# A two-block transformer on one core: roots by a GpSimd power and one Newton step, mask and residual adds on VectorE, norms at a higher priority

## The chip, the core and the metric

The kernel runs on one core of a Trainium2 chip. The core has a matrix engine (TensorE, PE in the profile), a vector engine (VectorE, DVE), an engine for activations and casts (ScalarE, ACT), GpSimd (POOL) and a sequencer that issues most of the loads (SyncE, SP). They run their own instruction queues in order and wait for each other by semaphores. The metric is the time of one execution on the device in microseconds (us), lower is better.

## The reference

The input is 256 tokens and 256 context tokens of 1024 features in float32. Two blocks run one after the other, and each has two layers:

```python
def first_block(...):                       # h_lat, h_ctx: [256, 1024] each
    for i in range(2):
        a = _modulate(_rms_norm(h, norm_mix[i]), m[0], m[1])
        o = _rwkv_mamba_mixer(a) if i == 0 else _neighbourhood_attention(a, rpb)
        h = h + m[2] * o
        t = _modulate(_rms_norm(h, norm_ffn[i]), m[3], m[4])
        h = h + m[5] * (_swiglu(t) if i == 0 else _moe_swiglu(t))   # 8 experts, top 2
    return _rms_norm(h_lat, norm_final)

def second_block(...):
    for i in range(2):
        u = modulate(h, sh1, sc1)           # layer norm, scale, shift
        y = (conv and differential attention if i == 0 else fourier_mix)(u) @ w
        h = layer_norm_affine(ALPHA * h + g1 * y, ln_g[i, 0], ln_b[i, 0])
        h = layer_norm_affine(ALPHA * h + g2 * sq_relu_mlp(modulate(h, sh2, sc2)),
                              ln_g[i, 1], ln_b[i, 1])
    return h
```

Each norm needs (x + eps) ** -0.5 for each token. In the neighbourhood attention a token sees a window of columns; outside it a mask takes the place of the bias.

## The kernel before

Tokens lie on the 128 partitions, so a residual h is four tiles of 128x1024 (two of context, two of tokens; after the attention only the last two go on). All products are done in three passes of single-precision parts (`mm3`, L231 to L233: high by high, low by high, high by low). Weights are loaded by SP into `raw` tiles of 128x1024; `split` makes the high part `wh` by a cast on ACT (L186) and the low part `wl` by a subtraction on DVE (L187). The same `split` makes xH and xL of the activations.

**A norm.** `norm_tile` (L416) squares the tile on ACT with a running sum `ms` (first block, L422), or takes mean and variance on DVE by `stats` (second block, L406 and L407), calls `rsqrt`, and scales the tile to `xn` on DVE (L423 or L426). `rsqrt` (L167) runs wholly on DVE: a first value from the bits (L173 to L175), then three Newton steps of two operations (L178 and L182; with n = 4 three operations, L180 to L182). With n = 1 it is nine operations of 128x1, each needing the one before. `xT` (L439) transposes two xn tiles on PE, applies scale and shift on the way out of PSUM (`xTf`, one half on ACT, the other on DVE, L453 and L454), and splits them. PE's first product of the next layer waits for that.

**Where norms stand after the mixer:** four at the mixer's end (`mixer_out`), four at the end of the first FFN (`l0_ffn`, w2 at f = 10), two at the attention's end, whose roots also scale the MoE's router, two for the context of the second block, `l1_end` (L1718) with two roots a tile, one root with n = 4 in the differential attention (L2086), and `post_norm` (L1914) with a layer norm in place and then the next layer's norm, two roots a tile, at three ends; at the last end of the program it has one root a tile.

**Adds on POOL.** In `l0_ffn` at f = 9 four tiles of 128x1024 are added to h (L1425). In `l1_attn`, `load_bias` (L1448) loads a `raw` tile of relative biases by 8 DMAs on SP, and POOL adds the mask `nam` (L1458), eight tiles in all; the mask comes by a DMA on POOL's queue (L1443). In `moe_pass`, after expert 6, POOL multiplies two accumulators by the gate (L1881) and adds them to h (L1882). POOL's queue also issues the loads of gates (L395) and of the rows `br` of ln_g and ln_b (L1901).

**What sets the order.** A scheduler places every engine's instructions by priority (in the main the order of the code; `high_priority` moves a stretch ahead by an offset) and by a simulated time at which operands are ready. On the engine they then run in exactly that order. Tiles come from pools with a fixed number of buffers; a new tile waits for the readers of the one that it replaces.

## Time and profile before

| | us |
|---|---|
| runs of the kernel before | 2846.43, 2853.15, 2857.51 |
| their median | 2853.15 |
| span of the profiled execution (first to last instruction) | 2849.6 |
| PE busy | 2636.1 (93%) |
| DVE busy | 1916.4 (67%) |
| ACT busy | 1286.7 (45%) |
| POOL busy | 191.2 (7%) |
| mean granted clock of PE | 0.945 of full speed |

The profile is of one execution. A timeline row begins with its start and its duration; "x5" is five instructions in a row, whose durations stand as one; the square bracket is the idle time of that engine before the row, and after the arrow stands the instruction whose end released it. A wait is idle time of an engine put down to the releaser that came last. Buffer numbers are left out of names: `xn`, `h`, `raw`, `sm` (any small tile). A wait costs time only on an engine that has nothing else to do.

### The profile page before, as it was taken

The page shows a single profiled execution, that of the slowest core. Times are in us where ns is not written, and L with a number is a line of the kernel's source. Part 1 is how long each engine was busy: PE and PEld are TensorE (multiplying, and loading weights), DVE is VectorE, ACT ScalarE, POOL GpSimd, SP SyncE. Part 2 cuts the span into 40 slices and gives each one's busy share as a digit, 9 for nine tenths or more (in the row PEclk, how much of TensorE's full clock was granted, in tenths as well). Part 3 has the DMA queues.
Part 4 walks back from the last instruction along what each step waited for, and adds up shares of the span by engine and source line. Part 5 has one row for each costly group of instructions (what it writes and reads, how often), then busy time and mean ns, then how long its engine had stood idle before and what let it go on. Part 6 is the DMA issues. An engine that isn't in the chain of part 4 may idle for free. (4 is left out here: it accounts for less than half of the span.)

```text
span 2849.6 us, 40766 instructions
## 1 busy us (share of the span) xinstructions
PE 2636.1 (93%) x15434; PEld 2092.5 (73%) x15434; DVE 1916.4 (67%) x3186; ACT 1286.7 (45%) x1760; POOL 191.2 (7%) x260
## 2 busy tenths in 40 slices
PE   6999899997999997999899999999997987996798
PEld 3775456654888886887788888888876766995797
DVE  4647778644544458345898988988896567556655
ACT  3532122112332223444688777778664443442343
POOL 0112223210000012000000000000010000000000
PEclk8999898888999998999899999999999998998899
DMA  6325776668333233333599999999986334653452
GB/s 235 93 67 177 256 243 208 196 226 296 97 96 96 89 92 87 103 91 108 198 375 349 342 350 345 361 359 333 367 315 228 113 96 141 188 182 99 155 185 74
DMA packets 324444, 570.83 MB, mean 200 GB/s; under 512 B 61752, under 2 KB 167608, under 8 KB 324240
## 3 DMA queue, kind: packets, MB, share of 16 engines
q1 hardware_dynamic: 304064, 544.61, 56.7%
q10 hardware_dynamic: 16784, 11.74, 1.4%
q0 software_dynamic: 3392, 11.80, 1.3%
q8 instruction: 123, 2.02, 0.3%
q14 instruction: 81, 0.66, 0.1%
HBM read 563.79 MB, written 4.28 MB: 199 GB/s over the span
## 5 line engine op out<-in xcount | busy, mean ns | idle before, releaser
L187 DVE TENSOR_TENSOR wl<-raw,wh 128x1024 fp32r<-128x1024 f32 x828 | 998.0, 1238 | 432.5 <-ACT wh L186 411.4
L186 ACT CAST wh<-raw 128x1024 fp32r<-128x1024 f32 x828 | 837.1, 1050 | 510.6 <-issue 193.0
L231 PE MATMUL ws<-xH,wh 128*128 128x256 f32 (+1 forms) x1392 | 458.5, 331 | 1.1 <-DVE xTf L454 0.8
L233 PE MATMUL ws<-xH,wl 128*128 128x256 f32 (+1 forms) x1392 | 457.3, 329 | 0.9 <-DVE wl L187 0.9
L232 PE MATMUL ws<-xL,wh 128*128 128x256 f32 (+1 forms) x1392 | 456.1, 328 | 0.5 <-DVE xL L187 0.5
L232 PE MATMUL mw<-wl,eH 128*128 128x512 f32 (+1 forms) x768 | 290.0, 378 | 2.6 <-DVE wl L187 2.4
L231 PEld LDWEIGHTS ws<-xH,wh 128*128 128x128 f32 x1392 | 265.5, 192 | 35.8 <-issue 10.1
L233 PEld LDWEIGHTS ws<-xH,wl 128*128 128x128 f32 x1392 | 265.1, 190 | 31.3 <-issue 6.8
L231 PE MATMUL mw<-wh,eH 128*128 128x512 f32 (+1 forms) x768 | 285.9, 375 | 1.1 <-ACT wh L186 1.1
L233 PE MATMUL mw<-wh,eL 128*128 128x512 f32 (+1 forms) x768 | 286.2, 373 | 0.0
L232 PEld LDWEIGHTS ws<-xL,wh 128*128 128x128 f32 x1392 | 265.3, 191 | 25.8 <-issue 2.5
L358 PE MATMUL ada<-raw,act 128*32 128x512 f32 x768 | 177.9, 734 | 33.3 <-DMA raw<-in_ada_w 12.8
L232 PEld LDWEIGHTS mw<-wl,eH 128*128 128x128 f32 x768 | 145.1, 189 | 35.0 <-DVE wl L187 11.0
L231 PEld LDWEIGHTS mw<-wh,eH 128*128 128x128 f32 x768 | 144.9, 189 | 27.2 <-ACT wh L186 2.0
L233 PEld LDWEIGHTS mw<-wh,eL 128*128 128x128 f32 x768 | 145.2, 189 | 24.2
L232 PE MATMUL y<-wl,uH 128*128 128x512 f32 x352 | 141.1, 401 | 4.0 <-DVE wl L187 4.0
L233 PE MATMUL y<-wh,uL 128*128 128x512 f32 x352 | 136.5, 392 | 0.0
L448 PE MATMUL xT<-ident,xn 128*128 128x128 f32 x160 | 36.7, 402 | 103.0 <-DVE xn L426 58.0
L231 PE MATMUL y<-wh,uH 128*128 128x512 f32 x352 | 115.5, 391 | 0.0
L448 PEld LDWEIGHTS xT<-ident,xn 128*128 128x128 f32 x160 | 29.7, 210 | 111.6 <-DVE xn L426 60.4
L358 PEld LDWEIGHTS ada<-raw,act 128*32 128x32 f32 x768 | 28.2, 123 | 110.8 <-issue 38.7
L231 PE MATMUL o<-wh,mH 128*128 128x512 f32 x256 | 100.0, 390 | 0.0
(475 smaller groups left out, 4182.8 us busy)
## 6 DMA issues: line engine op xcount, KB each, us to landing
raw<-in_moe_w SPq DMA_DIRECT2D x528, 512.0 KB
raw<-in_mlp_w SPq DMA_DIRECT2D x128, 512.0 KB
raw<-in_w_ada SPq DMA_DIRECT2D x96, 512.0 KB
raw<-in_ada_w SPq DMA_DIRECT2D x96, 512.0 KB
raw<-in_ffn_w SPq DMA_DIRECT2D x66, 512.0 KB
raw<-in_mix_w_in SPq DMA_DIRECT2D x24, 512.0 KB
raw<-in_na_w_qkv SPq DMA_DIRECT2D x24, 512.0 KB
raw<-in_w_in SPq DMA_DIRECT2D x24, 512.0 KB
```

The lines of the kernel that those rows point to most:

```text
L186: s.nc.scalar.copy(H, raw)
L187: s.nc.vector.tensor_tensor(L, raw, H, op=ALU.subtract)
L231: mm(out, lhsT=lH, rhs=rH, start=start, stop=False)
L232: mm(out, lhsT=lH, rhs=rL, start=False, stop=False)
L233: mm(out, lhsT=lL, rhs=rH, start=False, stop=stop)
L358: nc.tensor.matmul(ps[32 * j:32 * j + 32, :], lhsT=act[:, k, :], rhs=x[j // 2][:, j % 2 * 512:j % 2 * 512 + 512], start=(k == 0), stop=(k ...
L448: nc.tensor.transpose(p[:, j, t * 128:t * 128 + 128], xn[t][:, k * 128:k * 128 + 128], s.ident)
```

## The change

**Roots.** While the mixer runs, `rsqrt` is as before. After it, `x1 = x + eps` runs on DVE (L191), POOL raises it to the power -0.5 (L192, `tensor_tensor` with `pow` against a column of -0.5, set once by a memset), DVE makes `h = -0.5 * x1` (L193) and one Newton step (L195 and L199; with n = 4 three operations). So DVE has four operations instead of nine (n = 1), or five instead of twelve (n = 4), and five small tiles are used instead of three.

**Adds.** The four h adds of the FFN, the eight mask adds and the four operations after expert 6 go from POOL to DVE. A mask add is no longer issued with its load: it stands in `A(i)` at the first head of a group that uses the tile.

**Priorities.** `s.first()` puts at a priority 3000 ahead: the outputs of `xT` (now a function of their own, `xT_out`), the last gate adds and norms of mixer and FFN, `gate_alpha` and `post_norm`, and `l1_end`.

```diff
 def rsqrt(s, x, n, eps):
         v = s.nc.vector
+        if s.xp is not None:
...
+            return y
         y = s.small([128, n])[:, :n]
         a = s.small([128, n])[:, :n]
         h = s.small([128, n])[:, :n]
-        v.tensor_scalar(h, x, eps, -0.5, op0=ALU.add, op1=ALU.mult)
-        v.tensor_scalar(y.bitcast(I32), h.bitcast(I32), 1, None, op0=ALU.logical_shift_right)
-        v.tensor_scalar(y.bitcast(I32), y.bitcast(I32), -1.0, float(0x5F3759DF + 0x3FC00000), op0=ALU.mult, op1=ALU.add)
-        for _ in range(3):
...
+        x1 = s.small([128, n])[:, :n]
+        v.tensor_scalar(x1, x, eps, None, op0=ALU.add)
+        s.nc.gpsimd.tensor_tensor(y, x1, s.mhalf[:, 0:1].to_broadcast([128, n]), op=ALU.pow)
+        v.tensor_scalar(h, x1, -0.5, None, op0=ALU.mult)
+        if n == 1:
+            v.scalar_tensor_tensor(a, y, h, y, op0=ALU.mult, op1=ALU.mult)
+        else:
+            v.tensor_tensor(a, y, y, op=ALU.mult)
+            v.tensor_tensor(a, a, h, op=ALU.mult)
+        v.scalar_tensor_tensor(y, a, 1.5, y, op0=ALU.add, op1=ALU.mult)
         return y
+    def first(s):
+        return s.tc.high_priority(offset=NFIRST)
...
 def l0_ffn(s):
-                    nc.gpsimd.tensor_tensor(h[t], h[t], acc[t], op=ALU.add)
+                    v.tensor_tensor(h[t], h[t], acc[t], op=ALU.add)
...
 def l1_attn(s):
-            b2 = b.rearrange("p h r c -> p (h r) c")
-            nc.gpsimd.tensor_tensor(b2, b2, mask.unsqueeze(1).to_broadcast([128, 16, 64]), op=ALU.add)
+        def mask_bias(e, qt):
+            b2 = bias[e, qt].rearrange("p h r c -> p (h r) c")
+            v.tensor_tensor(b2, b2, mask.unsqueeze(1).to_broadcast([128, 16, 64]), op=ALU.add)
...
         def A(i):
+            if i % 4 == 0:
+                mask_bias(e, qt)
...
 def moe_pass(s, base):
-                            nc.gpsimd.tensor_tensor(acc[t], acc[t], s.gt2, op=ALU.mult)
-                            nc.gpsimd.tensor_tensor(s.h[t], s.h[t], acc[t], op=ALU.add)
+                            v.tensor_tensor(acc[t], acc[t], s.gt2, op=ALU.mult)
+                            v.tensor_tensor(s.h[t], s.h[t], acc[t], op=ALU.add)
...
 def mlp(s, i):
-                            s.gate_alpha(t, gate, ps[t][n], ns)
+                            with s.first():
+                                s.gate_alpha(t, gate, ps[t][n], ns)
                 if fs[-1] == 15:
-                    s.post_norm(i, 1, t, g, b)
+                    with s.first():
+                        s.post_norm(i, 1, t, g, b)
```

The first place is the way from the FFN to the attention. DVE before, from the last root of the fourth tile to the second half's first xTf (`sm` is the root, `sc` a scale, xL the low part that PE's second pass needs):

```order
L178 SCALAR_TENSOR_TENSOR sm_8916<-sm_8915,sm_8917 128x1
L454 TENSOR_SCALAR xTf_8963<-xT_8941,sc_8956,mcol_94 128x256
L182 SCALAR_TENSOR_TENSOR sm_8915<-sm_8916,sm_8915 128x1
L454 TENSOR_SCALAR xTf_8968<-xT_8946,sc_8956,mcol_94 128x256
L423 TENSOR_SCALAR xn_8912<-h_5950,sm_8915 128x1024
L454 TENSOR_SCALAR xTf_8973<-xT_8951,sc_8956,mcol_94 128x256
L187 TENSOR_TENSOR xL_8932<-xTf_8958,xH_8928 128x2x256
L187 TENSOR_TENSOR xL_8933<-xTf_8963,xH_8929 128x2x256
L187 TENSOR_TENSOR xL_8934<-xTf_8968,xH_8930 128x2x256
L187 TENSOR_TENSOR xL_8935<-xTf_8973,xH_8931 128x2x256
L454 TENSOR_SCALAR xTf_9135<-xT_9113,sc_9133,mcol_94 128x256
```

DVE after, from the last two xTf of the first half on:

```order
L482 TENSOR_SCALAR xTf_8946<-xT_8924,sc_8934,mcol_96 128x256
L482 TENSOR_SCALAR xTf_8951<-xT_8929,sc_8934,mcol_96 128x256
L1491 TENSOR_TENSOR raw_9133<-raw_9133,nam_8962 128x1024
L1491 TENSOR_TENSOR raw_9142<-raw_9142,nam_8962 128x1024
L1491 TENSOR_TENSOR raw_9519<-raw_9519,nam_8962 128x1024
L1491 TENSOR_TENSOR raw_9662<-raw_9662,nam_8962 128x1024
L1491 TENSOR_TENSOR raw_9955<-raw_9955,nam_8962 128x1024
L204 TENSOR_TENSOR xL_8910<-xTf_8936,xH_8906 128x2x256
L204 TENSOR_TENSOR xL_8911<-xTf_8941,xH_8907 128x2x256
L482 TENSOR_SCALAR xTf_9113<-xT_9091,sc_9111,mcol_96 128x256
L204 TENSOR_TENSOR xL_8912<-xTf_8946,xH_8908 128x2x256
```

The five mask adds now stand on DVE between the first half's xTf and its first xL, and the xTf of the second half stand between the xL of the first.

POOL at the same place before, from the gate's load on (L1425 the adds to h, `nam` the mask):

```order
L395 DMA gate_9175<-mrows_98 128x2x512
L1425 TENSOR_TENSOR h_5944<-h_5944,acc_6346 128x1024
L1425 TENSOR_TENSOR h_5946<-h_5946,acc_6347 128x1024
L1425 TENSOR_TENSOR h_5948<-h_5948,acc_6348 128x1024
L1425 TENSOR_TENSOR h_5950<-h_5950,acc_6349 128x1024
L1443 DMA nam_8984<-in_c_namask 128x64
L1458 TENSOR_TENSOR raw_9155<-raw_9155,nam_8984 128x1024
L1458 TENSOR_TENSOR raw_9165<-raw_9165,nam_8984 128x1024
```

POOL after:

```order
L414 DMA gate_9151<-mrows_100 128x2x512
L192 TENSOR_TENSOR sm_6276<-sm_6279,mhalf 128x1
L192 TENSOR_TENSOR sm_8797<-sm_8800,mhalf 128x1
L192 TENSOR_TENSOR sm_8830<-sm_8833,mhalf 128x1
L192 TENSOR_TENSOR sm_8863<-sm_8866,mhalf 128x1
L192 TENSOR_TENSOR sm_8896<-sm_8899,mhalf 128x1
L1474 DMA nam_8962<-in_c_namask 128x64
L414 DMA gate_11114<-mrows_100 128x2x512
```

The adds are gone; the mask's load now stands behind the powers of four norms (sm_8797 to sm_8896).

The second place is the MoE after expert 6. DVE before, from the last addition of expert 6's result on:

```order
L1863 TENSOR_TENSOR acc_11151<-cmb_18088,acc_11151 128x512
L187 TENSOR_TENSOR wl_18106<-raw_18103,wh_18105 128x1024
L187 TENSOR_TENSOR wl_18124<-raw_18121,wh_18123 128x1024
L187 TENSOR_TENSOR wl_18130<-raw_18127,wh_18129 128x1024
L187 TENSOR_TENSOR wl_18153<-raw_18150,wh_18152 128x1024
L1887 TENSOR_TENSOR mu_18145<-mw_18096,mu_18145 128x512
L187 TENSOR_TENSOR wl_18159<-raw_18156,wh_18158 128x1024
```

DVE after:

```order
L1898 TENSOR_TENSOR acc_11123<-cmb_18060,acc_11123 128x512
L204 TENSOR_TENSOR wl_18078<-raw_18075,wh_18077 128x1024
L204 TENSOR_TENSOR wl_18096<-raw_18093,wh_18095 128x1024
L1916 TENSOR_TENSOR acc_11122<-acc_11122,gate_11114 128x1024
L204 TENSOR_TENSOR wl_18102<-raw_18099,wh_18101 128x1024
L1916 TENSOR_TENSOR acc_11123<-acc_11123,gate_11114 128x1024
L204 TENSOR_TENSOR wl_18125<-raw_18122,wh_18124 128x1024
L1922 TENSOR_TENSOR mu_18117<-mw_18068,mu_18117 128x512
L204 TENSOR_TENSOR wl_18131<-raw_18128,wh_18130 128x1024
L1917 TENSOR_TENSOR h_5950<-h_5950,acc_11122 128x1024
L204 TENSOR_TENSOR wl_18149<-raw_18146,wh_18148 128x1024
L1917 TENSOR_TENSOR h_5952<-h_5952,acc_11123 128x1024
```

The four operations of 128x1024 now stand one by one between the splits of the next weights.

The third place is the end of a post norm in the second block. DVE before, from the second tile's layer norm to the root of its next norm:

```order
L1920 SCALAR_TENSOR_TENSOR h_5950<-h_5950,sm_26253,br_25318 128x1024
L406 BN_STATS st_26269<-h_5950 128x6 x2
L407 BN_AGGR mv_26268<-st_26269 128x2
L173 TENSOR_SCALAR sm_26275<-mv_26268 128x1
L174 TENSOR_SCALAR sm_26273<-sm_26275 128x1
L175 TENSOR_SCALAR sm_26273<-sm_26273 128x1
L178 SCALAR_TENSOR_TENSOR sm_26274<-sm_26273,sm_26275 128x1
L468 TENSOR_SCALAR sc_26310<-mcol_95 128x8
```

DVE after:

```order
L1955 SCALAR_TENSOR_TENSOR h_5952<-h_5952,sm_26191,br_25272 128x1024
L429 BN_STATS st_26204<-h_5952 128x6 x2
L430 BN_AGGR mv_26203<-st_26204 128x2
L191 TENSOR_SCALAR sm_26211<-mv_26203 128x1
L193 TENSOR_SCALAR sm_26210<-sm_26211 128x1
L195 SCALAR_TENSOR_TENSOR sm_26209<-sm_26208,sm_26210 128x1
L496 TENSOR_SCALAR sc_26242<-mcol_97 128x8
L199 SCALAR_TENSOR_TENSOR sm_26208<-sm_26209,sm_26208 128x1
L449 TENSOR_SCALAR xn_26202<-h_5952,mv_26203,sm_26208 128x1024
```

Four of the nine steps of the root are left, with a power on POOL between the first two and the last two.

## Rows read from the trace of the kernel before

**Rows 1.** The page's busy table: us, share of the span, instructions.

```profile
PE 2636.1 (93%) x15434; PEld 2092.5 (73%) x15434; DVE 1916.4 (67%) x3186; ACT 1286.7 (45%) x1760; POOL 191.2 (7%) x260
```

**Rows 2.** PE's waits: line, released by, us in total, times, longest.

```profile
PE xT L448 <- DVE xn L426: 58.0, 6, 15.3
PE xT L448 <- DVE sm L175: 17.9, 1, 17.9
```

**Rows 3.** Timeline of PE after the first FFN: start us, us, instruction, [idle before <-releaser].

```profile
1120.04 1.11 PE L448 MATMUL xT<-ident,xn 128*128 128x128 f32 x4 [17.94 <-DVE sm L175]
...
1131.88 0.37 PE L232 MATMUL ws<-xL,wh 128*128 128x256 f32 x1
```

**Rows 4.** Timeline of PE after the first post norm of the second block.

```profile
2376.25 1.11 PE L448 MATMUL xT<-ident,xn 128*128 128x128 f32 x4 [14.11 <-DVE xn L426]
2382.41 2.82 PE L448 MATMUL xT<-ident,xn 128*128 128x128 f32 x12 [5.05 <-DVE xn L426]
```

**Rows 5.** Stretches: length, busy us (count) of PE, PEld, DVE, ACT, POOL, PE clock, DMA share, GB/s.

```profile
1900.00:2080.00 180.00, 178.92 (x854) 147.82 (x853) 158.69 (x154) 135.09 (x161) 0.00 (x0) 1.00 0.99 357
2080.00:2110.00 30.00, 24.62 (x97) 18.33 (x96) 30.00 (x24) 16.83 (x20) 12.32 (x4) 0.89 0.75 249
...
1130.00:1340.00 210.00, 209.87 (x1343) 172.99 (x1342) 95.57 (x151) 92.71 (x186) 8.66 (x6) 1.00 0.35 98
740.00:1100.00 360.00, 360.00 (x1678) 302.32 (x1677) 178.47 (x211) 101.95 (x126) 10.44 (x4) 1.00 0.32 94
```

**Rows 6.** Timeline of POOL after the first FFN: mask adds.

```profile
1103.82 14.47 POOL L1458 TENSOR_TENSOR raw<-raw,nam 128x1024 f32<-128x1024 f32 x5 [1.85 <-DMA nam<-in_c_namask]
1186.06 2.40 POOL L1458 TENSOR_TENSOR raw<-raw,nam 128x1024 f32<-128x1024 f32 x1 [67.77 <-DMA raw<-in_na_rpb]
```

**Rows 7.** Timeline of DVE after the first FFN.

```profile
1103.80 1.22 DVE L187 TENSOR_TENSOR wl<-raw,wh 128x1024 fp32r<-128x1024 f32 x1
...
1105.00 2.77 DVE L1339 TENSOR_TENSOR h<-h,go 128x512 f32<-128x512 f32 x1
1107.69 3.36 DVE L187 TENSOR_TENSOR wl<-raw,wh 128x1024 fp32r<-128x1024 f32 x1
...
1113.89 2.11 DVE L178 SCALAR_TENSOR_TENSOR sm<-sm,sm 128x1 f32<-128x1 f32 x1
...
1131.28 2.03 DVE L454 TENSOR_SCALAR xTf<-xT,sc,mcol 128x256 f32<-128x256 f32 x4
```

**Rows 8.** POOL's groups by form: line, operation, shapes, count | busy us, mean ns | idle before.

```profile
L1458 POOL TENSOR_TENSOR raw<-raw,nam 128x1024 f32<-128x1024 f32 x8 | 21.6, 2719 | 112.9 <-DMA raw<-in_na_rpb 67.8 <-DVE PTs L1508 21.9 <-DMA raw<-in_na_w_qkv 21.4
...
L1075 POOL TENSOR_TENSOR Y<-Y,YM 64x256 f32<-64x256 f32 x16 | 11.7, 729 | 84.9 <-DVE YM L1067 54.7 <-DVE X L985 13.4 <-DVE sm L180 11.9
L1425 POOL TENSOR_TENSOR h<-h,acc 128x1024 f32<-128x1024 f32 x4 | 10.4, 2610 | 327.2 <-DVE acc L1424 323.7 <-issue 2.4 <-DMA raw<-in_na_rpb 1.2
...
L1882 POOL TENSOR_TENSOR h<-h,acc 128x1024 f32<-128x1024 f32 x2 | 6.7, 3350 | 0.0
...
L854 POOL COPY la<-Pi 128x4 f32<-128x4 f32 x16 | 2.6, 194 | 64.9 <-ACT Pi L850 64.9
```

**Rows 9.** Timeline of DVE in the MoE, around the adds after expert 6.

```profile
2086.49 12.98 DVE L187 TENSOR_TENSOR wl<-raw,wh 128x1024 fp32r<-128x1024 f32 x4
...
2100.00 4.62 DVE L187 TENSOR_TENSOR wl<-raw,wh 128x1024 fp32r<-128x1024 f32 x4
```

**Rows 10.** Timeline of DVE at the first post norm of the second block.

```profile
2366.64 0.15 DVE L174 TENSOR_SCALAR sm<-sm 128x1 int32<-128x1 int32 x1
...
2368.36 1.28 DVE L1920 SCALAR_TENSOR_TENSOR h<-h,sm,br 128x1024 f32<-128x1024 f32 x1
...
2379.63 0.15 DVE L173 TENSOR_SCALAR sm<-mv 128x1 f32<-128x1 f32 x1
...
2381.54 0.81 DVE L426 TENSOR_SCALAR xn<-h,mv,sm 128x1024 f32<-128x1024 f32 x1
```

More of the change, by code (lines that the diff above doesn't have):

```diff
@@ L169, in rsqrt @@
         v = s.nc.vector
+        if s.xp is not None:
+            y = s.small([128, n])[:, :n]
+            a = s.small([128, n])[:, :n]
+            h = s.small([128, n])[:, :n]
+            v.tensor_scalar(h, x, eps, -0.5, op0=ALU.add, op1=ALU.mult)
+            v.tensor_scalar(y.bitcast(I32), h.bitcast(I32), 1, None, op0=ALU.logical_shift_right)
+            v.tensor_scalar(y.bitcast(I32), y.bitcast(I32), -1.0, float(0x5F3759DF + 0x3FC00000), op0=ALU.mult, op1=ALU.add)
+            for _ in range(3):
+                if n == 1:
[5 more added lines that the diff above has]
+            return y
         y = s.small([128, n])[:, :n]
@@ L321, in startup @@
             s.act.append(t)
+        s.mhalf = cp.tile([128, 1], F32, name="mhalf")
+        nc.vector.memset(s.mhalf, -0.5)
         s.mcol = [cp.tile([128, 48, 2], F32, name=f"mcol{i}") for i in range(4)]
@@ L450, in xT, with xT_out @@
         sc, sh = mod()
+        with s.first() if s.banks is None else contextlib.nullcontext():
+            s.xT_out(ps, sc, sh, H, L, c0, put)
+    def xT_out(s, ps, sc, sh, H, L, c0, put):
+        nc = s.nc
         for i, p in enumerate(ps):
@@ L1352, in ev @@
             def ev(t, p):
-                s.gate_add(s.h[t], gc if t < 2 else gl, p, ns)
-                if n:
-                    s.dump("hm%d" % t, s.h[t])
-                    s.xn.append(s.norm_tile(s.h[t], "rms"))
+                with s.first() if n else contextlib.nullcontext():
+                    s.gate_add(s.h[t], gc if t < 2 else gl, p, ns)
+                    if n:
+                        s.dump("hm%d" % t, s.h[t])
+                        s.xn.append(s.norm_tile(s.h[t], "rms"))
             s.run(s.xstat(I["mix_w_out"], ns, oH, oL, range(4), ev, halves=n == 1))
@@ L1411, in w2 @@
                     else:
-                        s.gate_add(h[t], gt, p, ns)
+                        with s.first() if f == 10 else contextlib.nullcontext():
+                            s.gate_add(h[t], gt, p, ns)
                 if f == 10:
                     s.dump("hf%d" % t, h[t])
-                    s.xn.append(s.norm_tile(h[t], "rms"))
+                    with s.first():
+                        s.xn.append(s.norm_tile(h[t], "rms"))
         for f in range(11):
@@ L1931, in ev @@
             def ev(t, p):
-                s.gate_alpha(t, gate, p, ns)
-                if n:
-                    s.post_norm(i, 0, t, g, b)
+                with s.first() if n else contextlib.nullcontext():
+                    s.gate_alpha(t, gate, p, ns)
+                    if n:
+                        s.post_norm(i, 0, t, g, b)
             s.run(s.xstat(W, ns, oH, oL, range(2), ev, halves=n == 1))
```

17 lines of the change are left out of this document (10 added, 7 removed).

## The prediction

> **What bounds the kernel now.** I read the busy table first: TensorE (PE) is busy 93% of the span, VectorE (DVE) 67% [rows 1]; GpSimd (POOL) hardly works after the mixer. So a microsecond of DVE or POOL work counts only where PE stands still for it, and the list of PE's waits is the next view: 58.0 us in six waits for the normalized tile xn, and one of 17.9 us put down to a small tile of a root [rows 2]. Those are the ends of layers, where the norm of a finished residual is a chain on DVE that nothing else of PE's covers. Three places carry this change. At the end of the first FFN PE waits 17.94 us and gets its first full product only at 1131.88 [rows 3]; at each of three ends of a post norm it waits some 14 us and then 5 us [rows 4]; in the MoE, after expert 6, PE is busy 24.62 us of 30, against 178.92 of 180 in the stretch before [rows 5].
>
> **What makes the first of them so long.** While POOL runs five mask adds back to back (14.47 us from 1103.82) [rows 6], DVE instructions with two operands in SBUF stretch: a split's subtraction goes from 1.22 to 3.36 us, a residual add of half a tile to 2.77, a root's 128x1 step to 2.11 [rows 7]. The POOL adds stretch as well: 2.72 us in the mean for the mask adds and 3.35 us for the residual adds of the MoE, where one that runs alone takes 2.40 [rows 6, 8]. So here the two engines take turns. What moves an add from POOL to DVE therefore frees more DVE time than it costs: about 1.15 us (four subtractions of the same size in 4.62 us [rows 9]) against up to 2.1 (3.36 less 1.22).
>
> The Trainium skill ("SBUF — State Buffer", section "SBUF: two separate sides") says why: the port pair that DVE and GpSimd share is an exclusive lock, and a DVE operation with two SBUF inputs and a GpSimd operation that reads SBUF block each other for a whole instruction. The rows above agree (2.11 us for a 128x1 step). The same rule speaks against the other half of this change, since a power on POOL would hold DVE's two-input steps for as long as it runs. By the rule the three post norm ends give about 1.9 us each, without it 2.8, and the whole sum would be about 3 us better without it.
>
> **What one root costs, before and after.** Alone on DVE a root is nine dependent operations, 2379.63 to 2381.54, 1.91 us [rows 10], 0.21 each. The new one has four on DVE, of which the product with -0.5 lies beside the power, so three are in series (0.64), two hand-overs (PE follows DVE by 0.06 us: xn ends at 2382.35, PE starts at 2382.41 [rows 4, 10], so 0.12), and the power on POOL, X: 0.76 + X. The gain is 1.15 - X where a root stands alone. Where other DVE work fits between, only the operations count, and the gain is some 1.1 less what DVE's two-operand steps lose to the power. No row shows a power. From below X is bounded by the smallest POOL row, a copy of 128x4 at 0.19; from above by a whole 128x1024 add alone, 2.40 [rows 6, 8]. The operand is one element a partition, so it stands near the small end; the next row up, a two-operand operation of 64x256, takes 0.73 [rows 8]. A power is more than a copy and has 1/256 of that row's elements a partition: I take X = 0.5, about midway.
>
> **The change part by part**, at X = 0.5, as changes of the end time.
>
> *FFN to attention: -8.* Up to 1104.93 DVE does what it did. Then h (0.6, half of 1.22), a split (1.15), h (0.6): the last h is done at 1107.3 instead of 1113.7 [rows 7]. Tile 0's power is long back, so 0.64 and xn 0.8 follow [rows 10]; tile 1 has its power behind these, 1.15; tiles 2 and 3 stand alone, 2 x (0.76 + 0.5 + 0.8), with 0.4 for the two scales: 1114.4. ScalarE's squares keep up, since the order now has tile 2's ahead of two loads that wait for xn. Then four half xTf (0.51 each [rows 7]) to 1116.4. Now come the five mask adds that the order puts between these and the first xL: 5 x 1.15 = 5.75, to 1122.2; xL 0.6; PE's first xL product at 1122.9 for 1131.88 [rows 3]: -9. I give back 1, because two xTf of the second half now stand between the xL of the first (2 x 0.51): -8. Had the masks stayed behind the xL, it would be -14. The mask table's load is behind the fourth power on POOL; the adds now start 1.85 us after its issue [rows 6], so it should be there at about 1115, in time with 1 to spare, and a dearer X moves both.
>
> *Masks 6 to 8: +0.5 (0 to +4).* Each now stands in DVE's queue ahead of a softmax step. POOL waited for the sixth load until 1186.06 [rows 6]; now DVE would. In 1130 to 1340 PE is busy 209.87 of 210 us and DVE 95.57 [rows 5], so most of it is absorbed.
>
> *Adds after expert 6: -7 (-4 to -9).* Two gate products and two residual adds leave POOL for DVE. Now four subtractions take 12.98 us where they normally take 4.62 [rows 9], 8.4 lost; PE idles 5.4 of 30 us at a granted clock of 0.89, DMA drops from 357 to 249 GB/s [rows 5]. The stretch loses 30 x (1 - 249/357) = 9 us of loads in a stage that runs at 0.99 of DMA. In its place come 4 x 1.15 = 4.6 us of DVE, whose share is 88% there (158.69 of 180), interleaved one by one with splits. Of the lost 8.4 to 9, I leave 2 on the path. The cover for the rest is the spare 12% of DVE and the buffers loaded ahead; without it the gain is 4.
>
> *FFN adds at f = 9: 0.* POOL's four adds of 2.61 us (10.4 in all) [rows 8] go to DVE, 4.6 us, under products (740 to 1100: PE busy 360.00 of 360) [rows 5].
>
> *Mixer end to FFN: +0.8.* Four roots; the last tile's norm now waits for a power behind a gate's DMA on POOL, and no POOL add goes away here. Between -1 and +2.
>
> *Router: -1.3.* Two roots in line, of the kind timed above [rows 10]: 2 x (1.15 - 0.5).
>
> *MoE end: -2.1.* Four in line; two of them had other tiles' work between their steps, so I take 4 x (1.02 - 0.5).
>
> *Attention's n = 4 root: -0.7*, as one root alone.
>
> *Three post norm ends: 3 x -1.9 = -5.6.* Per end [rows 4, 10]: the first root's tail on DVE, 2366.64 to 2368.36 (1.72), becomes three steps (0.64), its power hidden: -1.1. The middle pair the same: -1.1. The last stands alone: -0.65. Two hidden powers hold DVE's two-operand steps as the mask adds do [rows 7], 0.5 each: +1.0. POOL's loads of ln_g and ln_b stand between the powers, but the one of ln_g starts when its buffer's reader on DVE ends, and xn of tile 0 (0.81) covers it.
>
> *Tail: -0.8*, two roots after the last product, one of them alone.
>
> *Priorities: 0.* The order shows the same neighbours on DVE apart from the dropped steps; the mixer is unchanged.
>
> The sum is -8 + 0.5 - 7 + 0.8 - 1.3 - 2.1 - 0.7 - 5.6 - 0.8 = -24.2. The profiled execution has a span of 2849.6, which would become 2825; the median of the runs is 2853.15, 3.5 above, so **2829**. About 21 powers lie on the path or hold DVE on it, so the sum moves by 21 us per us of X: -31 at X = 0.19, 0 at 1.65, +16 at 2.40.
>
> **Rivals.** *A dear power* (the other side): X of 2.0 or more at every norm. For it: no row prices a power, and POOL takes 0.73 us for 256 elements of a mere two-operand step [rows 8]. Against: one element a partition. At 2.40 it gives +16, 2869; it makes the kernel slower by over 0.5% from X = 2.3.
> *Masks on DVE hold attention*: the five adds wait for the table and 6 to 8 for their loads. Then FFN to attention gives -3 and the later ones +4: 2829 + 5 + 3.5, about 2838. For it: DVE works in order, and POOL did wait for the sixth load [rows 6]. Against: DVE is under half busy there.
> *The MoE gives nothing*: DVE at 88% cannot take 4.6 us more, and PE stands still as long as now: 2829 + 7 = 2836; with the masks too, 2845.
> *The roots stay exposed*: the steps are fewer, but where the order puts the Newton step right behind the product with -0.5, DVE idles through the power. At X = 1.0 this takes back half of the roots' gain: sum -14, 2839.
>
> **How the numbers follow.** About 0.5% (14 us, 2839 and 2867) is what a measurement of this kernel can tell from no change. Forecast 2829 (2819 to 2836): 0.55, faster. Masks: 0.13, split about evenly at 2839. MoE: 0.12, mostly faster. X near 1 or two rivals at once: 0.13, mostly the same. Dear power: 0.07, half slower by over 0.5%, and a loss from an unseen stall adds a little. That makes faster 0.68, same 0.25, slower 0.07. The range reaches from X = 0.19 with the MoE's best (-33 to -34, 2819) to two rivals at once (2845).
>
> **What would show it.** The power's own row on POOL (0.3 to 0.8 us) decides X. PE's wait at the FFN's end should fall from 17.9 to about 10 and its first xL product come some 9 us earlier after the last FFN product; DVE's five mask adds should stand there at 1.15 each. After expert 6 the subtractions should be 1.15 again and PE's idle time in 30 us fall from 5.4 to about 2. The waits of 14 and 5 us at the post norms should be some 1.3 and 0.6 shorter. I am wrong if the power takes over 1 us, if DVE idles ahead of a mask add, or if PE gains new waits inside attention.

## The result, and the profile after

The changed kernel takes 2821.16 us (median, 2819.58 to 2823.86); the kernel before took 2855.33 beside it on the same chip. The ratio is 0.9887, with a 95% interval of 0.9860 to 0.9914: 1.1% faster. The forecast was 2829, range 2819 to 2845. The profiled execution after has a span of 2818.1 us.

The page's busy table after, to be read beside [rows 1]:

```profile
PE 2632.0 (93%) x15434; PEld 2093.3 (74%) x15434; DVE 1885.5 (67%) x3039; ACT 1289.0 (46%) x1760; POOL 170.9 (6%) x276
```

DVE is 30.9 us less busy although it took over all the adds; POOL has more instructions (32 powers for 16 adds) and 20.3 us less work.

**Where the time went.** PE has 15434 instructions in every kernel here, so the time between two of its instructions of fixed number can be compared between traces. The stages below are cut so. PE's idle time is the stage's length less PE's busy time in the same window. Where the products are the same, what is left over is PE's own speed. The traces have two levels of the granted clock, full and half, so a mean of 0.84 is a mixture of them. Weighted by the granted clock at its time, PE's busy time at the router comes to 68.2 to 68.5 us at full clock in all fourteen traces here, though the stage takes 83.1 to 87.9: there the difference in speed is the clock's.

| stage (PE's instructions) | before | before, traced again | after | after less before | forecast |
|---|---|---|---|---|---|
| mixer (to 5010) | 727.83 | 720.37 | 721.22 | -6.6 | 0 |
| mixer end (to 5500) | 95.77 | 95.73 | 96.19 | +0.4 | +0.8 |
| FFN (to 6700) | 272.00 | 272.00 | 272.00 | 0 | 0 |
| FFN to attention (to 7100) | 84.23 | 84.21 | 75.52 | -8.7 | -8 |
| attention (to 8046) | 153.37 | 153.37 | 153.38 | 0 | +0.5 |
| router (to 8450) | 85.21 | 85.20 | 87.31 | +2.1 | -1.3 |
| experts to 6 (to 11400) | 620.94 | 621.12 | 621.13 | +0.2 | 0 |
| around the adds after expert 6 (to 11850) | 104.55 | 104.64 | 100.13 | -4.4 | -7 |
| MoE end and end of the layer (to 12400) | 123.27 | 123.13 | 116.56 | -6.7 | -2.1 |
| differential attention (to 12835) | 82.34 | 82.26 | 83.05 | +0.7 | -0.7 |
| first post norm (to 13160) | 74.21 | 74.18 | 71.49 | -2.7 | -1.9 |
| MLP and mixer of layer 1 (to 14000) | 129.18 | 129.18 | 129.18 | 0 | 0 |
| second post norm (to 14180) | 61.49 | 61.48 | 58.40 | -3.1 | -1.9 |
| third post norm (to 14500) | 74.02 | 74.01 | 72.31 | -1.7 | -1.9 |
| last MLP (to 15420) | 144.99 | 144.99 | 144.99 | 0 | 0 |
| tail | 16.22 | 16.22 | 15.24 | -1.0 | -0.8 |
| all but the mixer | 2121.8 | 2121.7 | 2096.9 | **-24.9** | **-24.2** |

The kernel before was traced a second time: behind the mixer it repeats within 0.2 us a stage, in the mixer it doesn't (7.5 us between two traces of one program). PE's idle time there scatters too (66.2 and 65.6 us before, 62.5 after, 61.8 in newton below, which has the old roots), and so does its busy time. So nothing shows that the mixer's -6.6 is the change's.

**FFN to attention.** PE after, then DVE, at the place of [rows 3, 7]:

```profile
1102.40 1.11 PE L471 MATMUL xT<-ident,xn 128*128 128x128 f32 x4 [6.48 <-DVE xn L446]
...
1115.64 0.58 PE L249 MATMUL ws<-xL,wh 128*128 128x256 f32 x1 [3.14 <-DVE xL L204]
```

```profile
1099.41 1.22 DVE L204 TENSOR_TENSOR wl<-raw,wh 128x1024 fp32r<-128x1024 f32 x1
1100.55 0.68 DVE L1367 TENSOR_TENSOR h<-h,go 128x512 f32<-128x512 f32 x1
...
1104.35 0.22 DVE L195 SCALAR_TENSOR_TENSOR sm<-sm,sm 128x1 f32<-128x1 f32 x1 [0.47 <-POOL sm L192]
...
1107.42 1.89 DVE L482 TENSOR_SCALAR xTf<-xT,sc,mcol 128x256 f32<-128x256 f32 x4
1109.23 5.75 DVE L1491 TENSOR_TENSOR raw<-raw,nam 128x1024 f32<-128x1024 f32 x5
1114.90 1.28 DVE L204 TENSOR_TENSOR xL<-xTf,xH 128x512 fp32r<-128x512 f32 x2
```

The wait of 17.94 us is 6.48; the split of 3.36 us is 1.22 and the residual add of 2.77 is 0.68. A new wait of 3.14 us stands at the first xL, behind the five mask adds of 1.15 each; the two together are 9.62, where the forecast had a wait of about 10.

**After expert 6.** The stretch around the adds, and the one before it, as in [rows 5] (length, busy of PE, PEld, DVE, ACT, POOL, clock, DMA share, GB/s):

```profile
1900.00:2060.00 160.00, 158.92 (x761) 131.15 (x760) 140.12 (x138) 119.46 (x140) 0.00 (x0) 1.00 0.98 353
2062.00:2092.00 30.00, 27.15 (x115) 20.39 (x115) 29.45 (x31) 23.04 (x27) 0.00 (x0) 1.00 0.88 288
```

PE idles 2.85 of 30 us where it idled 5.38, its clock stays full, and the loads go at 288 GB/s instead of 249.

**A post norm.** PE at the first of them, as in [rows 4]; then DVE and POOL from the first tile's layer norm to the last root:

```profile
2351.13 1.11 PE L471 MATMUL xT<-ident,xn 128*128 128x128 f32 x4 [12.00 <-DVE xn L449]
2357.31 2.82 PE L471 MATMUL xT<-ident,xn 128*128 128x128 f32 x12 [5.07 <-DVE xn L449]
```

```profile
2350.26 0.81 DVE L449 TENSOR_SCALAR xn<-h,mv,sm 128x1024 f32<-128x1024 f32 x1
2351.81 0.22 DVE L195 SCALAR_TENSOR_TENSOR sm<-sm,sm 128x1 f32<-128x1 f32 x1 [0.74 <-POOL sm L192]
...
2355.99 0.22 DVE L195 SCALAR_TENSOR_TENSOR sm<-sm,sm 128x1 f32<-128x1 f32 x1 [0.50 <-POOL sm L192]
```

```profile
2348.47 0.56 POOL L192 TENSOR_TENSOR sm<-sm,mhalf 128x1 f32<-128x1 f32 x1 [6.06 <-DVE sm L191]
2350.20 0.99 POOL L1936 DMA_DIRECT2D br<-in_ln_g  x1 [1.17 <-DVE sm L191]
2351.21 0.57 POOL L192 TENSOR_TENSOR sm<-sm,mhalf 128x1 f32<-128x1 f32 x1
```

The wait of 14.11 us is 12.00 (forecast: 1.3 shorter), and the wait of 5.05 has not changed (forecast: 0.6 shorter): the second tile's power stands behind the load of ln_g in POOL's queue, DVE idles 0.74 us for it, and that is what the last root gave.

**The power's price** is in POOL's groups by form (line, shapes, count, busy us, mean ns):

```profile
L192 POOL TENSOR_TENSOR sm<-sm,mhalf 128x1 f32<-128x1 f32 x30 | 20.9, 696 | 914.8 <-DVE sm L191 897.4 <-DVE mtop L1720 7.4 <-DVE sm L193 6.9
```

Alone it takes 0.55 to 0.58 us; the mean is higher because some are held up (below). The forecast took 0.5.

### The profile page after: what moved, and what is told of

Read it like the earlier page. It is cut to its first block, busy times and chain, and to the rows that moved or that the text cites. A ratio compares the mean times of both kernels' runs of the same rounds, so it can differ in the third digit from the quotient of the medians.

```text
span 2818.1 us, 40635 instructions
## 1 busy us (share of the span) xinstructions
PE 2632.0 (93%) x15434; PEld 2093.3 (74%) x15434; DVE 1885.5 (67%) x3039; ACT 1289.0 (46%) x1760; POOL 170.9 (6%) x276
## 5 line engine op out<-in xcount | busy, mean ns | idle before, releaser
L204 DVE TENSOR_TENSOR wl<-raw,wh 128x1024 fp32r<-128x1024 f32 x828 | 984.6, 1221 | 427.6 <-ACT wh L203 414.0
L249 PE MATMUL o<-wl,mH 128*128 128x512 f32 x256 | 99.9, 390 | 0.0
```

The source lines that it names most:

```text
L204: s.nc.vector.tensor_tensor(L, raw, H, op=ALU.subtract)
L249: mm(out, lhsT=lH, rhs=rL, start=False, stop=False)
```

## Experiments

All edits are to the changed kernel. "Outside the mixer" is the span of the traced execution less the mixer's stage: 2121.8 before, 2096.9 after. The times and ratios of whole kernels contain the mixer's scatter, so the parts are compared by stage.

### The parts, one at a time

**newton**: the old roots on DVE everywhere, all adds on DVE.

```diff
 def rsqrt(s, x, n, eps):
-        if s.xp is not None:
+        if True:
```

> The changed kernel with the roots alone undone: the old three Newton steps on VectorE after the mixer too; adds and masks stay on VectorE. Theory A (the sum of the prediction, root by root, with the price of 0.55 us that the trace after shows for a power): the roots' part is lost again, about 2 us at the end of the first FFN, 1 at the router, 2 at the end of the MoE, 0.5 in the attention of the second block, 2.2 at each of the three post norm ends and 1 in the tail, 13 us in all: 2834 us beside 2821. Rival B (the gain is that of the adds, and what the roots save is taken back by the wait for GpSimd): within 3 us of 2821.

Measured: 2839.21 us, ratio 0.9962 (0.9934 to 0.9990); outside the mixer 2111.2. So the adds alone give -10.6 (-5.6 at FFN to attention and -4.4 after expert 6), and the roots, given the adds, -14.3. FFN to attention takes 78.61 us, the stage after expert 6 100.13 as after, and the three post norm stages 74.21, 61.51 and 74.00 as before. But the router takes 87.86 us for 85.21 and the end of the MoE and of the layer 120.05 for 123.27, although the roots and adds of these two stages are those of the kernel before; of that more under "The scatter".

**masks_pool**: only the mask adds go back to POOL.

```diff
 def load_bias(e, qt):
+            b2 = b.rearrange("p h r c -> p (h r) c")
+            nc.gpsimd.tensor_tensor(b2, b2, mask.unsqueeze(1).to_broadcast([128, 16, 64]), op=ALU.add)
...
 def A(i):
-            if i % 4 == 0:
-                mask_bias(e, qt)
```

> The changed kernel with the mask adds alone back on GpSimd (in its queue they now stand behind the four powers of the first FFN's end). Theory A (VectorE's two-operand steps and GpSimd's adds take turns): the adds now fall on the eight xL instead of the roots, each xL takes up to 2.7 us instead of 0.6, and the way from FFN to attention is 3 to 9 us longer: about 2826 us beside 2821. Rival B: five adds of 1.15 us ahead of the first xL on VectorE cost as much as the contention, so the time stays within 2 us of 2821, or gets better by up to 5.7 us.

Measured: 2827.56 us, 0.9910 (0.9888 to 0.9931); outside the mixer 2097.9, only 1.0 above the changed kernel, which is rival B. FFN to attention takes 75.93 us, 0.4 more, although POOL's adds are back. That the median came near theory A's 2826 is the mixer's scatter (731.20 us for 721.22).

**roots_only**: all mask and residual adds back on POOL, the new roots kept.

> All mask adds and residual adds back on POOL, the roots as in the changed kernel. Theory (the parts are not additive: with powers in POOL's queue the order puts the mask adds behind the four powers, so that they no longer stretch DVE's chain): FFN to attention 76 to 77.5 us (75.5 with everything changed, 84.2 before, 78.6 with the adds alone), the two experts after expert 6 104.6 as before, all ends of post norms as in the changed kernel; outside the mixer about 9 us above the changed kernel, 15 below before. Rival (each part gives its own, the adds 5.6 at the FFN's end): FFN to attention about 81.

Measured: 2828.05 us, 0.9921 (0.9896 to 0.9947); outside the mixer 2103.8. FFN to attention takes 75.69 us, after expert 6 104.67. POOL, DVE and PE of roots_only between FFN and attention:

```profile
1103.89 0.55 POOL L192 TENSOR_TENSOR sm<-sm,mhalf 128x1 f32<-128x1 f32 x1 [1.38 <-DVE sm L191]
1104.39 0.58 POOL L1474 DMA_DIRECT2D nam<-in_c_namask  x1
1107.03 13.51 POOL L1489 TENSOR_TENSOR raw<-raw,nam 128x1024 f32<-128x1024 f32 x5 [2.05 <-DMA nam<-in_c_namask]
```

```profile
1107.44 5.29 DVE L204 TENSOR_TENSOR xL<-xTf,xH 128x512 fp32r<-128x512 f32 x2
```

```profile
1112.78 0.38 PE L249 MATMUL ws<-xL,wh 128*128 128x256 f32 x1 [1.36 <-DVE xL L204]
1115.55 0.39 PE L249 MATMUL ws<-xL,wh 128*128 128x256 f32 x1 [1.68 <-DVE xL L204]
1118.34 0.39 PE L249 MATMUL ws<-xL,wh 128*128 128x256 f32 x1 [1.33 <-DVE xL L204]
```

The engines still take turns: POOL needs 2.70 us a mask add, and two xL take 5.29 us where they took 1.28. But POOL now reaches the table's load only behind the four powers. So its adds no longer fall on the residual adds, splits and roots of the norm's chain; they fall on the xL, where PE has the products of the high parts to do meanwhile and waits 4.4 us in three pieces. The stage comes out as long as with DVE's five mask adds and their one wait of 3.14 us (75.69 and 75.52): PE idles 1.2 us more in it, and its mean granted clock is 0.93 for 0.89. **The parts do not add up**: here the roots alone give -8.5, the adds alone -5.6, both -8.7.

**moe_pool**: only the four operations after expert 6 go back to POOL.

```diff
 def moe_pass(s, base):
-                            v.tensor_tensor(acc[t], acc[t], s.gt2, op=ALU.mult)
-                            v.tensor_tensor(s.h[t], s.h[t], acc[t], op=ALU.add)
+                            nc.gpsimd.tensor_tensor(acc[t], acc[t], s.gt2, op=ALU.mult)
+                            nc.gpsimd.tensor_tensor(s.h[t], s.h[t], acc[t], op=ALU.add)
```

> The changed kernel with the four operations after expert 6 alone back on GpSimd. Theory A (they slow the splits by taking turns): 4 to 5 us longer, 2826 us beside 2821, with PE idle about 5 us of the 30 around them, as in the kernel before, and VectorE's four subtractions there at some 13 us. Rival B (the MoE makes up for it later): within 1.5 us of 2821.

Measured: 2833.00 us, 0.9932 (0.9910 to 0.9954). DVE beside POOL's four operations, as in [rows 9]:

```profile
2089.10 12.98 DVE L204 TENSOR_TENSOR wl<-raw,wh 128x1024 fp32r<-128x1024 f32 x4
```

The four splits take 12.98 us again, and the stage 104.65: +4.5. Of the other 3.7 us outside the mixer 3.1 stand at the end of the layer (100.45 us for 97.37 from PE's instruction 11960 to 12400), which takes 97.0 to 100.5 us in kernels with the same roots; of that more below.

### The power doubled

**pow2**: the power is computed twice, the second time into the same tile.

```diff
         s.nc.gpsimd.tensor_tensor(y, x1, s.mhalf[:, 0:1].to_broadcast([128, n]), op=ALU.pow)
+        s.nc.gpsimd.tensor_tensor(y, x1, s.mhalf[:, 0:1].to_broadcast([128, n]), op=ALU.pow)
```

> The changed kernel with each power done twice, so that a power costs 0.55 us more. Theory A of the prediction (about 21 powers lie on the path or hold VectorE on it): 21 x 0.55 = 11.5 us longer, 2833 us beside 2821. Rival B, from the trace after (VectorE's steps beside a power are not longer than elsewhere, it is the power that waits, up to 1.46 us; so only powers that VectorE waits for count, about 15): 8 us longer, 2829. Rival C (powers are hidden): within 2 us.

Measured: 2837.54 us, 0.9962 (0.9947 to 0.9977); outside the mixer 2107.4, +10.5. At 0.55 us a power that is worth 19 powers on the path, for the forecast's 21. The count is rough: the router (-3.0) and the end of the MoE and of the layer (+4.2) are in the sum, and kernels with equal roots there differ by about as much ("The scatter"); and the second powers take 0.55 to 1.66 us, since DVE's steps hold some of them. So 21 powers are not told from rival B's 15. What the run does show is that the shortness of the power matters: with two of them to a root, more than a third of the kernel's gain outside the mixer is gone.

### Where the five mask adds stand

**masks_late**: the table is made to depend on the first projected keys, so that the adds stand behind the eight xL. The passes of PE's first products follow each other in another order for it, which I had not expected; the mixer keeps its order.

```diff
 def A(i):
+            if i == 0:
+                v.scalar_tensor_tensor(mask, kT[0][:, 0, 0:64], 0.0, mask, op0=ALU.mult, op1=ALU.add)
             if i % 4 == 0:
                 mask_bias(e, qt)
```

> The changed kernel, but the mask table is made to depend on the first projected keys (one 128x64 step on DVE adds zero times kT to the table), so that DVE's five mask adds stand behind the eight xL instead of ahead of the first; the order of all else, the mixer's above all, stays as it is. Theory (the five adds, 5.75 us, are all that stands between the last xTf and xL): FFN to attention falls from 75.5 us to 69.8, PE no longer waits for xL there, everything else stays within 0.2 us outside the mixer; the attention itself stays at 153.4 although its first scores now wait for a table that is later by some 10 us. Rival (attention or ScalarE takes it back): FFN to attention plus attention falls by less than 3 us.

Measured: 2817.65 us, 0.9892 (0.9861 to 0.9922), as a whole not to be told from the changed kernel's 0.9887; outside the mixer 2090.9, 6.0 less. FFN to attention takes 70.74 us (-4.8), the attention 153.38. The other stages did not stay within 0.2 us as expected (router -4.2, end of the MoE and of the layer +2.3, second post norm +1.6). DVE and PE of masks_late, where the first xL now follows the xTf at once:

```profile
1110.50 1.90 DVE L482 TENSOR_SCALAR xTf<-xT,sc,mcol 128x256 f32<-128x256 f32 x4
1112.31 1.28 DVE L204 TENSOR_TENSOR xL<-xTf,xH 128x512 fp32r<-128x512 f32 x2
```

```profile
1111.10 2.82 PE L471 MATMUL xT<-ident,xn 128*128 128x128 f32 x12 [1.51 <-DVE xTf L482]
...
1115.29 0.36 PE L249 MATMUL ws<-xL,wh 128*128 128x256 f32 x1
```

PE does not wait for xL. The five adds were on the path, for 4.8 of their 5.75 us, and the attention hides them.

**masks_early**: the table's load stands in the code at f = 5 of the FFN and has a buffer of its own, so that the adds can run under the FFN.

```diff
 def l0_ffn(s):
             if f == 5:
+                s.nam = s.np.tile([128, 64], F32, name="nam")
+                nc.gpsimd.dma_start(s.nam, I["c_namask"])
...
 def l1_attn(s):
-        mask = s.row(nm="nam")[:, 0:64]
-        nc.gpsimd.dma_start(mask, I["c_namask"])
+        mask = s.nam
```

> The mask table is loaded under the FFN into a buffer of its own, so that DVE can make the first five mask adds under the FFN's products instead of between the transposed tiles (xTf) and the first xL. Theory (the five adds stand on the path, 5 x 1.15 = 5.75 us): the stretch from the end of the FFN to attention falls from 75.5 us to about 70, and the step from the last h to PE's first xL product from 15.1 us (1100.55 to 1115.64) to 9.4. Rival (something else ends just as late there, ScalarE's squares or the split's other operand): the stretch stays within 1.5 us of 75.5. All later stages as in the changed kernel. The mixer's own order also shifts with the new buffer, so it is compared by stage.

Measured: 2871.73 us, 1.0081 (1.0056 to 1.0107): slower than before. FFN to attention takes 70.87 us, as the theory said, and the FFN 1.05 more: DVE waits 5.08 us for a bias tile ahead of a mask add there, and PE then 0.74 for DVE. The loss is in the mixer, 777.23 us, whose instructions stand in another order. The table's load, which now waits for no reader of an older tile, did not stay in the FFN; POOL of masks_early:

```profile
3.49 0.70 POOL L1453 DMA_DIRECT2D nam<-in_c_namask  x1
```

A program with the same buffer and the load at its old place in the code gets the same orders, and one with the load at f = 5 in one of the old buffers keeps the mixer's; neither was run, so what the second is worth is open. The mixer's window in the traces of before, before traced again, the changed kernel and masks_early (columns as in [rows 5]):

```profile
0.00:727.83 727.83, 661.67 (x5010) 421.93 (x5011) 452.90 (x1248) 190.64 (x330) 134.90 (x224) 0.90 0.59 197
```

```profile
0.00:720.37 720.37, 654.82 (x5011) 420.18 (x5012) 451.78 (x1248) 190.33 (x330) 134.85 (x224) 0.91 0.60 199
```

```profile
0.00:721.22 721.22, 658.70 (x5010) 421.73 (x5011) 450.86 (x1239) 190.41 (x330) 135.13 (x227) 0.90 0.60 199
```

```profile
0.00:777.23 777.23, 697.74 (x5011) 444.65 (x5012) 448.73 (x1239) 190.65 (x330) 135.35 (x228) 0.85 0.55 185
```

PE's idle time there (length less busy) is 66.2, 65.6, 62.5 and 79.5 us; the rest of the loss is PE's busy time, 39.0 us more than after for the same products, at a granted clock of 0.85 for 0.90. Weighted by the clock it is no longer than after (591.6 us at full clock, and 595.4).

### What is left in a root

**pow_only**: four DVE steps of each root go.

```diff
 def rsqrt(s, x, n, eps):
         s.nc.gpsimd.tensor_tensor(y, x1, s.mhalf[:, 0:1].to_broadcast([128, n]), op=ALU.pow)
-        v.tensor_scalar(h, x1, -0.5, None, op0=ALU.mult)
-        if n == 1:
-            v.scalar_tensor_tensor(a, y, h, y, op0=ALU.mult, op1=ALU.mult)
...
-        v.scalar_tensor_tensor(y, a, 1.5, y, op0=ALU.add, op1=ALU.mult)
         return y
```

> Leaves out the Newton step: the root is POOL's power alone, and its result is used as it is. Of each root four DVE steps go, three of them in series (0.64 us by the rows). Theory (the root is a chain in series, and what is left of it after the power counts in full where a root stands alone): every end of a post norm gets about 1.3 us shorter (two roots of three in line), the n=4 root 0.6, router and tail 0.6 to 1.3 each, FFN to attention 1.5 or so, in all 7 to 9 us below the changed kernel outside the mixer. Rival (what ends last at the post norms is POOL's load of ln_g and ln_b, issued ahead of the power): the ends of the post norms stay within 0.5 us, and the whole gives 3 us or less.

Measured: 2805.61 us, 0.9837 (0.9808 to 0.9866); outside the mixer 2082.1, 14.8 below the changed kernel, twice what was expected. PE of pow_only at the first post norm, and POOL there:

```profile
2349.36 1.11 PE L462 MATMUL xT<-ident,xn 128*128 128x128 f32 x4 [10.90 <-DVE xn L440]
2353.97 2.82 PE L462 MATMUL xT<-ident,xn 128*128 128x128 f32 x12 [3.49 <-DVE xn L440]
```

```profile
2347.16 2.19 POOL L190 TENSOR_TENSOR sm<-sm,mhalf 128x1 f32<-128x1 f32 x2 [5.41 <-DVE sm L189]
2348.95 0.58 POOL L1927 DMA_DIRECT2D br<-in_ln_g  x1
```

The waits are 1.1 and 1.58 us shorter (expected 1.3 in all). The second is more than the steps left out: without the Newton step the second tile's power stands ahead of the load of ln_g, and DVE's 0.74 us of idle time goes as well. The three post norm stages give 6.8 of the 14.8 us. The largest single piece is FFN to attention, 70.79 us for 75.52, where 1.5 was expected. There the order of DVE has changed too, and one xL stands ahead of the five mask adds:

```profile
1114.00 0.68 DVE L195 TENSOR_TENSOR xL<-xTf,xH 128x512 fp32r<-128x512 f32 x1
1114.60 5.76 DVE L1482 TENSOR_TENSOR raw<-raw,nam 128x1024 f32<-128x1024 f32 x5
```

So most of that piece is what masks_late gives (70.74), and not the price of the Newton step.

**ln_act**: the loads of ln_g, ln_b and the final weight go to ScalarE's queue, with the Newton step kept.

```diff
-        s.nc.gpsimd.dma_start(t, bass.AP(tensor=src.tensor, offset=src.offset, ap=[[0, 128], [1, 1024]]))
+        s.nc.scalar.dma_start(t, bass.AP(tensor=src.tensor, offset=src.offset, ap=[[0, 128], [1, 1024]]))
```

> Loads of ln_g, ln_b and the final norm's weight are issued from ScalarE's queue instead of POOL's, so that no DMA issue stands ahead of a power. Theory (the 0.74 us for which DVE waits for POOL's first power at 2351.81 is the issue of the load at 2350.20, 0.99 us long): PE's first wait at an end of a post norm falls from 12.0 to about 11.3 us, and the second from 5.05 to about 4.5, so 1 to 1.3 us for each of three ends. Rival (the power itself, or the hand-over, is what DVE waits for): 12.0 and 5.05 stay within 0.2. A second rival: ScalarE is itself on the path there, and the issue in its queue costs what it saves, 0 or up to 1 us more.

Measured: 2823.07 us, 0.9894 (0.9863 to 0.9925), no gain in the whole. PE of ln_act at the first post norm, and DVE and POOL at the root in question:

```profile
2368.07 1.11 PE L471 MATMUL xT<-ident,xn 128*128 128x128 f32 x4 [12.00 <-DVE xn L449]
2373.55 2.82 PE L471 MATMUL xT<-ident,xn 128*128 128x128 f32 x12 [4.37 <-DVE xn L449]
```

```profile
2368.09 0.22 DVE L195 SCALAR_TENSOR_TENSOR sm<-sm,sm 128x1 f32<-128x1 f32 x1
```

```profile
2367.11 0.94 POOL L192 TENSOR_TENSOR sm<-sm,mhalf 128x1 f32<-128x1 f32 x1 [1.15 <-DVE sm L191]
```

The idle time ahead of that step is gone, and the second wait is 0.70 us shorter at each of three ends (5.07 to 4.37, 5.05 to 4.36, 5.06 to 4.37). So the load in the queue was the cause. The first wait did not move: my expectation put the 0.74 us ahead of the wrong tile. Yet the three stages are only 0.4, 0.2 and 0.2 us shorter, for PE's clock in two of them fell (0.85 to 0.82, 0.88 to 0.86), and FFN to attention was 1.4 and the end of the layer 3.0 us longer.

**pow_late** joins pow_only and masks_late; **pow_late_ln** adds ln_act to that.

> Leaves out the Newton step, as pow_only did, with the mask adds behind xL, as in masks_late. Theory (the two are in series on the same chain): FFN to attention 65 us (70.8 with the power alone, less 5.75), all else as pow_only; 2800 us in all, 15 outside the mixer below the changed kernel plus 5. Rival (with the chain that short, ScalarE's squares or PE's transposes end last there): 68 to 70 us.

Measured: 2811.91 us, 0.9863 (0.9831 to 0.9894). FFN to attention takes 70.31 us, against 70.79 in pow_only: not the theory's 65, and by another way than the rival's. In pow_only one xL already stands ahead of the five adds, and PE, busy from 1112.78 without a wait of 0.4 us, has the products of the high parts to cover them. The two edits do not add up.

> As pow_late, and the loads of ln_g, ln_b and the final weight from ScalarE's queue. Theory (without the Newton step the first two powers already stand ahead of the load in POOL's queue, so no power waits for a load there any more): equal to pow_late at the ends of the post norms within 0.3 us each. Rival (the load still costs): about 0.7 us less at each of three ends, as with the Newton step.

Measured: 2808.63 us, 0.9845 (0.9813 to 0.9876). The three post norm stages are 68.66, 56.99 and 69.89 us for 68.67, 56.87 and 69.83: with the power ahead of the load already, moving the load gives nothing, as the theory said.

### The scatter

**before_again**: the kernel before, traced once more.

> The kernel before, unchanged, traced a second time. Theory (the 6.6 us by which the mixer of the changed kernel was shorter in its profiled execution are the scatter of TensorE's granted clock there, since its instruction order is the same): the mixer's stretch differs from 727.8 us by several us, while every stretch behind it repeats within 0.5 us, but for those that follow a load of the modulation weights (router, end of layer 1), where up to 3 us of clock come and go. Rival (the changed kernel shortens the mixer): 727.8 within 1 us.

Measured: the second column of the table; the mixer 720.37 us for 727.83. All kernels here but masks_early leave the mixer's order as it was, and their mixer takes 719.9 to 736.3 us. The theory holds, and more than it said: router and end of the layer, which I had taken for scatter, repeat in the same kernel within 0.15 us. They differ between kernels whose chains there are the same. The router's window before, after and in masks_late:

```profile
1333.20:1418.41 85.21, 74.97 (x405) 65.35 (x405) 67.17 (x139) 50.09 (x70) 1.14 (x2) 0.88 0.49 165
```

```profile
1318.31:1405.62 87.31, 78.83 (x406) 69.24 (x405) 64.42 (x119) 50.65 (x70) 3.58 (x6) 0.84 0.48 163
```

```profile
1316.61:1399.73 83.12, 75.38 (x406) 66.19 (x405) 64.38 (x119) 50.25 (x70) 3.59 (x6) 0.88 0.50 172
```

PE's idle time falls from 10.24 to 8.48 us with the change, and its busy time rises from 74.97 to 78.83 for the same products, at 0.84 for 0.88. In masks_late, with the same chain at the router, the clock is 0.88 again and the stage 83.12. Nor do the roots decide: newton, with the old roots, takes 87.86 us there, 78.4 of them busy, and pow2, with the longer roots, 84.31. The end of the MoE and of the layer takes 116.2 to 120.7 us in the kernels with the Newton root, 120.05 with the old roots in newton and 123.3 before. So a difference of 3 us between two kernels in either stage shows nothing of the change. What sets the clock's level so is left open.

**The best of them** is pow_only, 2805.61 us against 2821.16 for the changed kernel; their intervals (0.9808 to 0.9866, and 0.9860 to 0.9914) hardly overlap, and outside the mixer it is 14.8 us shorter. pow_late (2081.9 outside the mixer) and pow_late_ln (2085.3) lie with it.

## Why the prediction was right, point by point

The mechanism was right where the runs tested it: the power is short, POOL's adds no longer stretch DVE's steps, and the chains at the ends of layers are shorter. The sum outside the mixer was -24.2, and -24.9 was measured. That it is so near is luck in part: half of the terms were near, and the largest errors (+3.4 at the router, +2.6 after expert 6, -4.6 at the end of the MoE and of the layer) cancelled. The median came lower (2821 for 2829); between the two profiled executions another 6.6 us went in the mixer, which the forecast did not have and the change is not shown to have made.

- **The power, X = 0.5**: 0.55 alone, so the dear power did not come. The slope fits too, roughly: 10.5 us for 0.55 (pow2).
- **FFN to attention, -8**: -8.7, for the reasons given. With the 6.2 us by which the last FFN product ended earlier, the steps fell where the forecast had put them: last h done at 1101.2 (forecast 1101.1), first xL at 1114.9 (1116.0). "Had the masks stayed behind the xL, it would be -14": masks_late gives -13.5 there. What I missed is that the roots alone would do it (roots_only, -8.5), since POOL's queue then holds the masks back.
- **Masks 6 to 8, +0.5**: 0. DVE did wait for the loads, up to 3.21 us ahead of a mask add, which the forecast had named as a sign of being wrong; the attention took no longer, so the sign was too strict.
- **After expert 6, -7**: -4.4, the term that was mis-sized. I had sized the loss by DVE's stretched splits (8.4 us) and the loads not made (9 us). But PE idled 5.38 us there, and that with its slower clock was all there was to get back: 2.85 us of idle time stay, and the clock is full. moe_pool shows the same 4.5 the other way.
- **Router, -1.3**: PE's idle time fell by 1.8, its busy time rose by 3.9 at the lower clock: +2.1. The forecast left the clock's scatter out here, which is larger than the term. Against newton, which has the same low clock with the old roots, PE idles 1.0 us less and the stage is 0.6 shorter.
- **MoE end, -2.1**: -6.7. PE's idle time at the end of the layer fell by 2.7 (20.91 to 18.19), near the forecast, but it is 19.20 in newton without the new roots, so only 1.0 of it is shown to be theirs. The other part is busy time, PE's speed, and it differs between kernels (97.0 to 100.5 us for the 97.37 of it with the same roots).
- **n = 4, -0.7**: idle time -0.7 (10.95 to 10.25), but the stage +0.7: PE's busy time is 1.4 us longer at the same mean clock (0.94), so this is not the clock, and its cause is open.
- **Post norms, -1.9 each**: PE's waits fell by 2.1, 2.2 and 2.2, and the stages by 2.7, 3.1 and 1.7, the clock making up the difference (the second takes 60.0 us, not 58.4, in roots_only, masks_pool and masks_late). Near, but two steps in it failed. The +1.0 for powers that hold DVE did not come (below). And "xn of tile 0 covers" the load of ln_g was wrong: [rows 10] gave 0.81 us of cover, the load's issue took 0.99 and the power 0.57 behind it. ln_act shows that it cost 0.70 at each end.
- **Mixer end, FFN adds, tail, priorities**: +0.4 for +0.8, 0 for 0, -1.0 for -0.8; the priorities move nothing: with the offset at 0 in place of 3000 the built program is the same to the last instruction.

**The lock.** [rows 7] and roots_only (xL 0.64 to 2.65 us beside mask adds) bear out what the Trainium skill says in "SBUF — State Buffer", section "SBUF: two separate sides": the engine that started first holds the pair that the two share for its whole instruction. For the power, only one direction was seen. POOL and DVE of the changed kernel ahead of the second post norm:

```profile
2539.68 1.46 POOL L192 TENSOR_TENSOR sm<-sm,mhalf 128x1 f32<-128x1 f32 x1 [183.72 <-DVE sm L191]
```

```profile
2539.45 1.27 DVE L1954 SCALAR_TENSOR_TENSOR h<-h,mv,br 128x1024 f32<-128x1024 f32 x1
```

The power starts 0.23 us behind DVE's step and waits for its end. The other way round, in pow_only the first power starts at 2347.16, and DVE's step, 0.15 us later, is not longer for it:

```profile
2347.31 1.27 DVE L1945 SCALAR_TENSOR_TENSOR h<-h,mv,br 128x1024 f32<-128x1024 f32 x1
```

Yet not every power that starts first goes through. One that starts 0.08 us ahead of an xn ends only with that xn:

```profile
1101.51 0.87 POOL L192 TENSOR_TENSOR sm<-sm,mhalf 128x1 f32<-128x1 f32 x1 [4.98 <-DVE sm L191]
```

```profile
1101.59 0.75 DVE L446 TENSOR_SCALAR xn<-h,sm 128x1024 f32<-128x1024 f32 x1
```

Ahead of the steps at L1954, which read two whole tiles (h and ln_g), starting 0.04 to 0.15 us first was enough at the three ends (0.56 us); why an xn differs is open. So a power of 128x1 waits, and was not seen to hold anything; the measurement decides against my +1.0.

## What to carry to other kernels

Price the end of a stage by the idle time of the bounding engine there; a stretched engine that isn't the bound, or bytes not loaded, overstate what can be won (4.4 for 7 here). Before adding up the parts of a change, ask of each what the queue's order would be without the others: two parts that free the same chain are worth little more than one. And when a step moves to another engine, read that engine's queue for what stands ahead of it, DMA issues included.
